# A hybrid decoder trunk: products of two head pairs issued in turn, and a queue of its own for the gate products

## The chip, the cores and the metric

The kernel runs on one core of one Trainium2 chip. The metric is the device time of one execution in microseconds, smaller is better. The time before is the median of three runs. One further execution was profiled, and all rows below come from that one.

## The reference, cut to what matters

Two residual layers over 512 positions and a width of 2048. Each layer normalises x, multiplies it by one wide input matrix, feeds slices of the result to four mixers, multiplies the mixers' outputs by a gate, and projects back.

```python
def layer(x):
    h = rms_norm(x); p = h @ w_in              # 52 column blocks of 128
    y = concat(mla(p), s5(p), rwkv7(p), diff_attention(p))   # 4 x 512 wide
    return x + (y * silu(gate(p))) @ w_out     # 2048 x 2048

def rwkv_step(state, r, w, k, v, a, b):        # 8 heads of 64, one state 64 x 64 each
    sa = state @ a
    state = state * w + sa[:, None] * b + v[:, None] * k
    return state, state @ r
```

## The kernel before, in words

**Layout.** Features lie on partitions, the 512 positions on the free axis. Every large product is split into three float32r products (high and low part of each side, helper `three`, line 258 on): TensorE sees 128x128 weights and 512 columns. Small products are plain float32, which TensorE runs as two instructions each. The profile shows all products on line L126 and all transposes on L130, the two methods of `Clock`.

**Order on TensorE.** The class `Clock` writes TensorE's order out by hand. It counts a modelled time from the columns issued. The filler is the stream of big products: `in_proj` (52 column blocks of 16 steps per layer), then `partial` (output blocks over the first 12 of 16 inner steps, taken from the list `PART`, while the attention is still running), then `out_proj` (the rest). Small work is generators: each `yield 6.0` says that its next piece is due 6 modelled us later, and `Clock.run` slips it into the filler when it is due. The generators are `recurrent` (the RWKV heads), `others` (S5 tables, S5, GLU, the latent attention, the differential attention) and, in `out_proj` of the first layer, `tables` for the second one.

**Order on the other engines.** A scheduler orders DVE, ACT, POOL and the DMA issues of SP by priority in a simulated time. On the chip each of these queues runs strictly in order. Weights come through `weights`: a DMA into `raw`, an ACT copy to `wh` (L242), a DVE subtraction to `wl` (L243), with three buffers of each, at high priority. `late(i)` keeps an ACT or DVE instruction behind the latest such weight split.

**Chunk products of RWKV** (`rwkv_two`). A pass `d` handles two head pairs, `s` = 0 and 1. Pair `s` keeps its operands on partitions `TS[s]`, 0 to 63 or 64 to 127. Within a pair there are two heads `h`. For each `(s, h)` the keys BK of eight chunks are written by DVE (L598, L599) into one buffer, then 8 products of 64x128 keys with 128 columns of Q are issued in two halves `j`, each followed by two masked copies out of PSUM by DVE (L608, L610), then 8 transposes of BK, copied out by ACT (L615). The one buffer makes the second head's keys wait until the first head's products are done.

**Gate products.** The gate block is scaled out of PSUM (L1449), goes through tanh (L1450, L1451) and is either multiplied at once (`mix`) or, when the mixers are not yet there, stored to DRAM (gD, `early`) and loaded again by `mix_one`. `mix` loads the mixer output y into the one buffer `zr` (L1461), POOL multiplies (L1462), ACT writes the high part MH (L1463), DVE the low part ML (L1464). `mixing` calls `mix_one` at every fourth step of the filler.

**Sums of squares.** `sum_sq` squares on ACT (L469) and adds on POOL (L471). `absorb` calls it for every output block of the first layer and also writes the next layer's XH (L462) and XL (L463). `out_proj` walks the blocks m = 0 to 15 in order. A block that `partial` has begun has 4 inner steps left, another one 16.

Of the kernel before, what the change touches and what calls it, by code (L numbers as in the profile page):

```python
# [187 lines left out]
def trunk(ctx, tc, io, KT=16, depth=DEPTH):  # L188
# [45 lines left out]

    def weights(pl, src, n, bufs, first=0, into=None):

        w = WCOL
        with tc.high_priority(offset=first) if first else ExitStack():
            raw = pl.tile([128, w], F32, tag="raw", name="raw", bufs=bufs[0])
            SP.dma_start(out=raw[:, :n], in_=src)  # L240
            wh, wl = into or (pl.tile([128, w], F32R, tag=t, name=t, bufs=bufs[1]) for t in ("wh", "wl"))
            x = A.copy(out=wh[:, :n], in_=raw[:, :n])  # L242
            y = V.tensor_sub(out=wl[:, :n], in0=raw[:, :n], in1=wh[:, :n])  # L243
# [35 lines left out]
    def small(pl, srcs, nk, rh, rl, done, bufs=(1, 2)):  # L279

        nxt = weights(pl, srcs[0], nk * 128, bufs)
        for j in range(len(srcs)):
            wh, wl = nxt
            if j + 1 < len(srcs):
                nxt = weights(pl, srcs[j + 1], nk * 128, bufs)
# [53 lines left out]
    def s5_tables(pl, l, pace):  # L339
# [76 lines left out]
        for q in range(4):  # L416
# [38 lines left out]
            SP.dma_start(out=s5tab[l, q], in_=cs2.rearrange("p a g q -> p a (g q)"))  # L455


    def absorb(sp, k, x, pvt, sqs, eng=G):
# [5 lines left out]
        sum_sq(sp, sqs, x, k == 0, eng)  # L464

    def sum_sq(lp, sqs, src, first, eng=G):

        sq = sqs if first else lp.tile([128, S], F32, name="sq", tag="sq", bufs=2)[:, :src.free_size()]
# [40 lines left out]
    def rwkv_two(rp, P, l, d, lo_, z, yD):  # L509
# [12 lines left out]
        Qs, BKts, SVs, bvs, nDs = [], [], [], [], []  # L522
        for s in range(2):
# [68 lines left out]

            for h in range(2):
                hs = TS[h]
                if h == 0:
                    yield 6.0
                BK = rp.tile([128, 8, 128], F32, name="BK", tag="BK", bufs=1)
                late(V.tensor_tensor(out=BK[T, :, T], in0=c3(b)[hs], in1=c3(Ei)[hs], op=ALU.mult))  # L598
                late(V.tensor_tensor(out=BK[T, :, B], in0=c3(k2)[hs], in1=c3(Ei)[hs], op=ALU.mult))  # L599
                yield Y["bk0"] - 5.0 if h == 0 else Y["bk1"]  # L600
                for j in range(2):
                    s4 = slice(8 * h + 4 * j, 8 * h + 4 * j + 4)
                    ps = pb()
                    for i in range(4):
                        PE.matmul(ps[:, i * 128:(i + 1) * 128], lhsT=BK[T, 4 * j + i, :],
                                  rhs=Q[T, 8 * h + 4 * j + i, :], start=True, stop=True)
                    ps3 = ps.rearrange("p (c t) -> p c t", t=128)
                    V.tensor_tensor(out=NM[T, s4, :], in0=ps3[T],  # L608
                                    in1=maskS[T].unsqueeze(1).to_broadcast([64, 4, 128]), op=ALU.mult)
                    V.tensor_tensor(out=Q[B, s4, :], in0=ps3[B],  # L610
                                    in1=maskS[B].unsqueeze(1).to_broadcast([64, 4, 128]), op=ALU.mult)
                ps = pb()
                for c in range(8):
                    PE.transpose(ps[:, c * 64:(c + 1) * 64], BK[T, c, :], ident[T, T])
                A.copy(out=BKt[:, 8 * h:8 * h + 8].rearrange("p c f -> p (c f)"), in_=ps)  # L615
            nD = dram(f"nD{l}{p}", [64, 16, 64])
            SP.dma_start(out=nD, in_=NM[T, :, 0:64])
            nDs.append(nD)
# [9 lines left out]
            Qs.append(Q), BKts.append(BKt), SVs.append(SV), bvs.append(bvD)  # L628

# [263 lines left out]
    def s5_glu(gp, l, P, uD, ysD, out):  # L893
# [12 lines left out]

        nxt = load(0)
        for t in range(4):
# [27 lines left out]
        yield from small(gp, [io["w_glu"][l, t] for t in range(4)], 4, GH, GL, done)  # L936
# [32 lines left out]
    def low_rank_col(pl, sqs, n, rxc, name, mul):  # L969
# [3 lines left out]
        yield 9.0  # L973
# [11 lines left out]
    def load_split(pl, src, n, P, g, name):  # L985
# [12 lines left out]
        for t in range(n):  # L998
# [9 lines left out]
            if t + 2 < n:  # L1008
                rs.append(load(t + 2))
                yield 4.0  # L1010
        return xh, xl, sqs

    def mla_kv(pa, l, P, aD, rxc, knD, vtD):
        def at():
            return pa.tile([128, S], F32, name="at", tag="at", bufs=3)

        kh, kl, ksq = yield from load_split(pa, aD[0:2], 2, P, "kvg", "ck")
# [9 lines left out]
        yield from small(pa, [io["w_uk"][l, h] for h in range(4)], 2, kh, kl, done)  # L1027
        ws = [weights(pa, io["w_uv"][l, :, k * 512:k * 512 + 512], 512, (1, 2)) for k in range(2)]
# [10 lines left out]
    def mla_q(pa, l, P, aD, rxc, qnD, qrD):  # L1039
        qh, ql, sqs = yield from load_split(pa, aD[3:7], 4, P, "qg", "cq")  # L1040
# [3 lines left out]
        order = (4, 5, 0, 1, 2, 3)  # L1044
# [7 lines left out]
        yield from small(pa, [io["w_uq"][l, j] for j in order], 4, qh, ql, done)  # L1052
# [28 lines left out]
    def mla_att(pd, qc, qn, qnD, qrD, knD, kpD, vtD, out):  # L1081
        def raw(src):
            t = pd.tile([128, S], F32, name="raw", tag="raw", bufs=3)
# [15 lines left out]
        def head(h):  # L1099
            if h == 0:  # L1100
                r = raw(kpD)
                yield Y["ld"]
                hd["kp"] = split("kp", r)
                load(0)
                yield Y["ld"]
# [680 lines left out]
```

## Time and profile before

| | us |
|---|---|
| median of three runs | 2024.81 |
| lowest and highest | 2019.72, 2025.67 |
| the profiled execution, its own time | 2023.16 |
| its span | 2021.4 |

The profiled execution took 1.76 us more than its span, and lies 1.65 us below the median. Busy times of TensorE overlap: a 512-column product is shown with about 390 ns and the next one begins about 230 ns later. A gap is therefore read from one start to the next. The mean granted TensorE clock over the execution is 0.982 of full speed.

### The profile page before, as it was taken

To read this page: it belongs to the slowest core of one execution; us is meant where nothing else is said; L and a number is where in the kernel's file an instruction comes from. 1 tells how busy PE (TensorE), PEld (TensorE's weight loads), DVE (VectorE), ACT (ScalarE), POOL (GpSimd) and SP (SyncE) were. 2 spreads that over 40 slices of the span, in tenths; PEclk is the share of its full clock that TensorE was granted. 3 is DMA by queue.
4 is the path that set the end of the run, shared out by engine and by line. 5 is a ranking of instruction groups with operands and counts; after the bars stand their busy time and mean duration, and the time that the engine had idled before them with its cause. 6 is when DMAs were issued, how large, how long until landed. Compare 5 with 4: busy or idle time off the path is not lost.

```text
span 2021.4 us, 31452 instructions
## 1 busy us (share of the span) xinstructions
PE 1955.9 (97%) x10975; PEld 1596.9 (79%) x10975; DVE 1303.5 (64%) x2801; ACT 831.8 (41%) x1734; POOL 368.4 (18%) x422
## 2 busy tenths in 40 slices
PE   9979999999999999998999999999999998999997
PEld 7767877788888787886788888778787787887787
DVE  6886866546776577649646686664683675766442
ACT  5543434344234355434433233443332353554351
POOL 1112203123001122004101111312210112200122
PEclk9989989999999999998999999999999999999998
DMA  5453545455462455455642445365456437445553
GB/s 209 142 167 117 144 119 148 155 169 171 151 214 95 146 179 172 154 171 179 203 133 93 136 119 155 96 194 170 160 158 172 150 100 224 131 145 167 159 175 116
DMA packets 241422, 311.08 MB, mean 154 GB/s; under 512 B 83312, under 2 KB 109168, under 8 KB 241264
## 3 DMA queue, kind: packets, MB, share of 16 engines
q1 hardware_dynamic: 241120, 308.91, 49.3%
q8 instruction: 86, 1.41, 0.3%
q14 instruction: 72, 0.59, 0.1%
q10 hardware_dynamic: 144, 0.17, 0.0%
HBM read 235.75 MB, written 70.88 MB: 152 GB/s over the span
## 4 chain that ended last, share of the span: by engine, by line
PE 77%; DMA 8%; DVE 7%; ACT 3%; issue 2%; POOL 1%; SPq 1%; DVEq 0%; POOLq 0%; ACTq 0%
PE acc L126 57%; PE pb L126 18%; PE pb L130 2%; DVE wl L243 1%; DMA zr<-yD 1%; POOL stg L1462 1%; DMA raw<-in_w_out_dram 1%; DMA raw<-qkD 1%; ACT K L850 1%; DMA raw<-in_w_in_dram 1%; DMA T<-K 1%; DMA qs<-qrD 0%; SPq L854 0%; DMA xo<-xP 0%; DMA gD<-stg 0%
## 5 line engine op out<-in xcount | busy, mean ns | idle before, releaser
L126 PE MATMUL acc<-XH,wl 128*128 128x512 f32 x1600 | 654.8, 409 | 20.3 <-DVE zr L504 10.7
L126 PE MATMUL acc<-XL,wh 128*128 128x512 f32 x1600 | 629.9, 394 | 1.1 <-DVE XL L463 1.1
L126 PE MATMUL acc<-XH,wh 128*128 128x512 f32 x1600 | 629.9, 394 | 0.0
L242 ACT CAST wh<-raw 128x512 fp32r<-128x512 f32 (+1 forms) x560 | 342.4, 616 | 563.9 <-PE acc L126 415.9
L243 DVE TENSOR_TENSOR wl<-raw,wh 128x512 fp32r<-128x512 f32 (+1 forms) x560 | 395.3, 710 | 257.5 <-ACT wh L242 253.1
L126 PEld LDWEIGHTS acc<-XH,wl 128*128 128x128 f32 x1600 | 303.8, 190 | 95.2 <-DVE zr L504 11.2
L126 PEld LDWEIGHTS acc<-XH,wh 128*128 128x128 f32 x1600 | 303.1, 189 | 66.0
L126 PEld LDWEIGHTS acc<-XL,wh 128*128 128x128 f32 x1600 | 304.1, 190 | 60.7 <-DVE XL L463 2.7
L126 PE MATMUL acc<-MH,wl 128*128 128x512 f32 x448 | 180.9, 404 | 12.5 <-DVE xo L1545 10.1
L126 PE MATMUL acc<-ML,wh 128*128 128x512 f32 x448 | 176.5, 394 | 0.2 <-DVE ML L1464 0.2
L126 PE MATMUL acc<-MH,wh 128*128 128x512 f32 x448 | 176.5, 394 | 0.0
L703 POOL TENSOR_SCALAR tmp<-SV,ec 64x64 f32<-64x64 f32 x112 | 69.8, 625 | 339.8 <-DVE SV L730 171.7
L126 PEld LDWEIGHTS acc<-MH,wl 128*128 128x128 f32 x448 | 85.3, 190 | 32.7 <-DVE xo L1545 11.8
L126 PEld LDWEIGHTS acc<-MH,wh 128*128 128x128 f32 x448 | 85.0, 190 | 18.3
L126 PEld LDWEIGHTS acc<-ML,wh 128*128 128x128 f32 x448 | 85.3, 190 | 16.5 <-DVE ML L1464 0.5
L1462 POOL TENSOR_TENSOR stg<-stg,zr 128x512 f32<-128x512 f32 x32 | 45.7, 1428 | 178.3 <-DMA zr<-yD 67.4
L471 POOL TENSOR_TENSOR sqs<-sqs,sq 128x512 f32<-128x512 f32 (+1 forms) x32 | 42.3, 1321 | 133.6 <-ACT sq L469 133.5
L1279 POOL TENSOR_TENSOR sr<-ss,cc 128x1 f32<-128x1 f32 x32 | 21.8, 686 | 188.0 <-DVE ss L1277 178.2
L955 ACT ACTIVATE pt<-pb,nb,fc 128x128 f32<-128x128 f32 (+3 forms) x64 | 39.5, 618 | 32.9 <-DVE nb L954 32.5
L640 DVE TENSOR_TENSOR tmp<-X 64x30 f32<-64x30 f32 (+14 forms) x120 | 39.2, 326 | 11.0 <-DMA X<-nD 5.1
L953 DVE TENSOR_REDUCE mx<-pb 128x1 f32<-128x128 f32 (+3 forms) x96 | 45.9, 478 | 0.5
L1463 ACT ACTIVATE MH<-stg 128x512 fp32r<-128x512 f32 x32 | 20.1, 631 | 57.3 <-POOL stg L1462 50.5
(398 smaller groups left out, 2908.6 us busy)
## 6 DMA issues: line engine op xcount, KB each, us to landing
raw<-in_w_in_dram SPq DMA_DIRECT2D x416, 256.0 KB, 3.4
raw<-in_w_out_dram SPq DMA_DIRECT2D x128, 256.0 KB, 3.4
zr<-yD SPq DMA_DIRECT2D x32, 256.0 KB, 2.9
gD<-stg SPq DMA_DIRECT2D x22, 256.0 KB, 3.3
stg<-gD SPq DMA_DIRECT2D x22, 256.0 KB, 3.4
zD<-stg SPq DMA_DIRECT2D x18, 256.0 KB, 3.1
xP<-stg SPq DMA_DIRECT2D x18, 256.0 KB, 2.1
xo<-xP SPq DMA_DIRECT2D x18, 256.0 KB, 3.4
```

The lines of the kernel that those rows point to most:

```text
L126: return self.nc.tensor.matmul(out, lhsT=lhsT, rhs=rhs, **kw)
L130: return self.nc.tensor.transpose(out, in_, identity)
L242: x = A.copy(out=wh[:, :n], in_=raw[:, :n])
L243: y = V.tensor_sub(out=wl[:, :n], in0=raw[:, :n], in1=wh[:, :n])
L471: eng.tensor_tensor(out=sqs, in0=sqs, in1=sq, op=ALU.add)
L640: i = V.tensor_tensor(out=t2, in0=X[:, 0:j, j:j + 1].to_broadcast([64, j, n]), in1=X[:, j:j + 1, j + 1:32].to_broadcast([64, j, n]), op=AL ...
L703: G.tensor_scalar(out=T1[T, h], in0=SVs[s][T, c, h], scalar1=ec[T, h, c:c + 1], scalar2=None, op0=ALU.mult)
L850: A.copy(out=K[:, g], in_=ps[32 * g:32 * g + 16, 0:128])
L953: V.tensor_reduce(out=mx, in_=ps[:, 0:n], axis=AX.X, op=ALU.max)
L955: A.activation(out=pt, in_=ps[:, 0:n], func=AF.Exp, scale=fcol[:, qb:qb + 1], bias=nb, accum_out=sm)
L1279: G.tensor_tensor(out=sr, in0=ss, in1=C("mhalf", 0, 1), op=ALU.pow)
L1462: G.tensor_tensor(out=g, in0=g, in1=y, op=ALU.mult)
```

## The change

1. **Chunk products.** The products of both head pairs are taken out of the loop over `s` and issued after both pairs are prepared, in turn: pair 0, pair 1, pair 0, and so on, into two PSUM banks. The transposes likewise. The keys of the second head get a place of their own: that of the states SV, which are not needed yet.
2. **Gate products.** `mix`, `open_mix`, `mix_one` and `mixing` go. A generator `mixer` takes their place. Every gate block is stored to DRAM. The mixer loads y and gate for up to two tiles into four buffers, and 9 modelled us later issues the product on DVE, then MH and ML as before. `partial` now runs until all 16 tiles are mixed.
3. **Sums of squares** are added on DVE everywhere.
4. **Order of `out_proj`** in the first layer: full blocks and begun blocks alternate.
5. **Small weights** (`small`, `mla_kv`) are loaded two ahead and early, and split only when due. Some due times are shorter: 9 to 6 in `low_rank_col`, 4 to 3 in `load_split`, one wait of 9 less at the first attention head, tables at a pace of 3.0 in place of 4.5 in the second layer and of 2.5 in place of 3.0 in the first, with one pause more per quarter before their store.

```diff
+    def small(pl, srcs, nk, rh, rl, done, raws):
+        def split(j):
+            wh, wl, x, y = split_w(pl, raws[j], nk * 128, 2)
+            late(x)
+            if j + 2 < len(srcs):
+                raws.append(load_w(pl, srcs[j + 2], nk * 128, 2))
+            return wh, wl
...
-            SP.dma_start(out=s5tab[l, q], in_=cs2.rearrange("p a g q -> p a (g q)"))
+            yield pace
+            late(SP.dma_start(out=s5tab[l, q], in_=cs2.rearrange("p a g q -> p a (g q)")))
...
         if not first:
-            eng.tensor_tensor(out=sqs, in0=sqs, in1=sq, op=ALU.add)
+            V.tensor_tensor(out=sqs, in0=sqs, in1=sq, op=ALU.add)
...
+            yield 4.0
+            Ks.append((BK, SV.rearrange("p c h v -> p c (h v)")))
             for h in range(2):
                 hs = TS[h]
-                if h == 0:
-                    yield 6.0
-                BK = rp.tile([128, 8, 128], F32, name="BK", tag="BK", bufs=1)
-                late(V.tensor_tensor(out=BK[T, :, T], in0=c3(b)[hs], in1=c3(Ei)[hs], op=ALU.mult))
-                late(V.tensor_tensor(out=BK[T, :, B], in0=c3(k2)[hs], in1=c3(Ei)[hs], op=ALU.mult))
-                yield Y["bk0"] - 5.0 if h == 0 else Y["bk1"]
...
+                late(V.tensor_tensor(out=Ks[s][h][T, :, T], in0=c3(b)[hs], in1=c3(Ei)[hs], op=ALU.mult))
+                late(V.tensor_tensor(out=Ks[s][h][T, :, B], in0=c3(k2)[hs], in1=c3(Ei)[hs], op=ALU.mult))
...
+        yield 5.0
+        for h in range(2):
+            for j in range(2):
+                s4 = slice(8 * h + 4 * j, 8 * h + 4 * j + 4)
+                pss = pb(), pb()
+                for i in range(4):
+                    for s, T in enumerate(TS):
+                        PE.matmul(pss[s][:, i * 128:(i + 1) * 128], lhsT=Ks[s][h][T, 4 * j + i, :],
+                                  rhs=Qs[s][T, 8 * h + 4 * j + i, :], start=True, stop=True)
+                for s, T in enumerate(TS):
+                    B = TS[1 - s]
+                    ps3 = pss[s].rearrange("p (c t) -> p c t", t=128)
+                    V.tensor_tensor(out=NM[T, s4, :], in0=ps3[T],
+                                    in1=maskS[T].unsqueeze(1).to_broadcast([64, 4, 128]), op=ALU.mult)
+                    V.tensor_tensor(out=Qs[s][B, s4, :], in0=ps3[B],
+                                    in1=maskS[B].unsqueeze(1).to_broadcast([64, 4, 128]), op=ALU.mult)
+                yield 2.6
+            pss = pb(), pb()
+            for c in range(8):
+                for s, T in enumerate(TS):
+                    PE.transpose(pss[s][:, c * 64:(c + 1) * 64], Ks[s][h][T, c, :], ident[T, T])
...
+            if h == 0:
+                yield 1.0
...
-        yield 9.0
+        yield 6.0
...
-            G.tensor_tensor(out=g, in0=g, in1=y, op=ALU.mult)
...
+        def mixer(self, mctx):
+            l, on, n = self.l, [], 0
+            yield from self.need(("rwkv",))
...
+            while len(self.mixed) < 16:
+                t = next((t for t in self.gates if (l, "y", t) in PE.done), None)
+                if t is not None and len(on) < 2:
+                    self.gates.remove(t)
+                    (a, x), (b, z) = (((zp, "zr"), (cp, "w2a2")), ((mp, "y"), (cp, "lo")))[n % 2]
+                    y, g = (q.tile([128, S], F32, name=w, tag=w, bufs=1) for q, w in ((a, x), (b, z)))
+                    SP.dma_start(out=y, in_=self.yD[t])
+                    SP.dma_start(out=g, in_=self.gD[t])
+                    on.append((PE.t + Y["ld"], t, y, g))
+                    n += 1
+                elif on and on[0][0] <= PE.t:
+                    _, t, y, g = on.pop(0)
+                    late(V.tensor_tensor(out=g, in0=g, in1=y, op=ALU.mult))
+                    A.mul(out=self.MH[:, t], in_=g, mul=0.5)
+                    V.scalar_tensor_tensor(out=self.ML[:, t], in0=g, scalar=0.5, in1=self.MH[:, t],
+                                           op0=ALU.mult, op1=ALU.subtract)
+                    self.mixed.add(t)
+                yield 1.5
...
             for m in PART:
-                if (l, "others") in PE.done:
+                if len(self.mixed) == 16:
                     break
...
-            for m in range(KT):
+            order, rest = [], [m for m in range(KT) if m not in self.part]
+            for j, m in enumerate(rest):
+                order += [m] + self.part[j * len(self.part) // len(rest):(j + 1) * len(self.part) // len(rest)]
+            for m in order:
...
+                PE.spawn(L.mixer(mctx), 2)
```

## Rows read from the trace of the kernel before

**Rows 1.** The page's first part: busy us, share of the span, instructions.
```profile
PE 1955.9 (97%) x10975; PEld 1596.9 (79%) x10975; DVE 1303.5 (64%) x2801; ACT 831.8 (41%) x1734; POOL 368.4 (18%) x422
```

**Rows 2.** TensorE's waits: waiting line, releaser, us in total, times, longest.
```profile
PE acc L126 <- DVE zr L504: 10.7, 1, 10.7
PE acc L126 <- DVE xo L1545: 10.1, 4, 4.6
...
PE pb L126 <- DVE BK L599: 1.9, 1, 1.9
```

**Rows 3.** Stretches: PE, PEld, DVE, ACT, POOL busy; granted clock; DMA share; GB/s.
```profile
98.00:120.00 22.00, 11.27 (x41) 8.80 (x38) 17.10 (x30) 13.93 (x23) 4.58 (x6) 0.69 0.41 137
146.00:157.00 11.00, 9.12 (x38) 6.83 (x38) 7.20 (x11) 1.20 (x2) 1.66 (x2) 0.69 0.55 160
...
760.00:772.00 12.00, 7.74 (x28) 6.24 (x27) 8.82 (x26) 5.36 (x15) 4.00 (x4) 0.72 0.58 182
928.00:973.00 45.00, 33.80 (x126) 25.99 (x127) 45.00 (x117) 20.66 (x44) 10.35 (x6) 0.89 0.58 180
...
1694.00:1724.00 30.00, 23.49 (x92) 18.48 (x92) 17.53 (x27) 13.78 (x26) 9.01 (x6) 0.89 0.71 221
```

**Rows 4.** TensorE's groups of instructions for the chunk products and transposes.
```profile
L126 PE MATMUL pb<-Q,BK 64*128 64x128 f32 x256 | 33.2, 281 | 1.9 <-DVE BK L599 1.9
...
L130 PE MATMUL pb<-cc,BK 64*128 64x64 f32 x128 | 10.8, 227 | 0.0
```

**Rows 5.** TensorE in order of time, one head's chunk products: start, us, instructions.
```profile
139.14 2.05 PE L126 MATMUL pb<-Q,BK 64*128 64x128 f32 x16
141.03 0.65 PE L130 MATMUL pb<-cc,BK 64*128 64x64 f32 x8
141.61 0.50 PE L126 MATMUL acc<-XH,wl 128*128 128x512 f32 x1
```

**Rows 6.** TensorE in order of time: two products on partition halves, then one on all.
```profile
97.61 1.13 PE L126 MATMUL pb<-lo,w2a 64*128 64x512 f32 x4
...
477.60 1.12 PE L126 MATMUL pb<-rk,cc 128*128 128x512 f32 x2
```

**Rows 7.** All engines in order of time, a stretch of the first layer's output projection.
```profile
942.55 1.44 POOL L471 TENSOR_TENSOR sqs<-sqs,sq 128x512 f32<-128x512 f32 x1 [0.88 <-ACT sq L469]
942.75 1.79 DVE L463 SCALAR_TENSOR_TENSOR XL<-xo,pvt,XH 128x512 fp32r<-128x512 f32 x1
...
946.36 0.74 DVE L463 SCALAR_TENSOR_TENSOR XL<-xo,pvt,XH 128x512 fp32r<-128x512 f32 x1
```

**Rows 8.** All engines in order of time, gate products of the first layer.
```profile
754.98 1.28 POOL L1462 TENSOR_TENSOR stg<-stg,zr 128x512 f32<-128x512 f32 x1 [3.68 <-DMA zr<-yD]
756.29 0.63 ACT L1463 ACTIVATE MH<-stg 128x512 fp32r<-128x512 f32 x1 [3.30 <-POOL stg L1462]
...
766.16 0.58 PE L126 MATMUL pb<-dVT,PT 128*128 128x128 f32 x1 [4.26 <-ACT PT L965]
```

**Rows 9.** DVE's groups of instructions.
```profile
L610 DVE TENSOR_TENSOR Q<-pb,cc 64x512 f32<-64x512 f32 x32 | 22.0, 688 | 0.6
...
L1464 DVE SCALAR_TENSOR_TENSOR ML<-stg,MH 128x512 fp32r<-128x512 f32 x32 | 21.9, 688 | 30.7 <-ACT MH L1463 30.6
```

**Rows 10.** POOL's groups of instructions, shapes apart.
```profile
L1462 POOL TENSOR_TENSOR stg<-stg,zr 128x512 f32<-128x512 f32 x32 | 45.7, 1428 | 178.3 <-DMA zr<-yD 67.4 <-DVE ss L1277 24.4 <-DMA stg<-gD 21.8
L471 POOL TENSOR_TENSOR sqs<-sqs,sq 128x512 f32<-128x512 f32 x26 | 37.9, 1456 | 114.9 <-ACT sq L469 114.7
```

**Rows 11.** DMA issues: engine, count, KB each, median us to landing.
```profile
raw<-in_w_in_dram SPq DMA_DIRECT2D x416, 256.0 KB, 3.4
...
gD<-stg SPq DMA_DIRECT2D x22, 256.0 KB, 3.3
```

**Rows 12.** All engines in order of time, the query compression's sum of squares.
```profile
487.74 2.98 POOL L1007 TENSOR_TENSOR sqs<-sqs,rw 128x512 f32<-128x512 f32 x2 [1.97 <-ACT rw L1006]
...
498.65 0.95 PE L126 MATMUL pb<-cc,sqs 128*128 128x2 f32 x8
```

More of the change, by code (lines that the diff above doesn't have):

```diff
@@ L232, in trunk, with load_w, split_w @@
     s5b = dram("s5b", [depth, 4, 128, 2, 2, 64])
-    def weights(pl, src, n, bufs, first=0, into=None):
[L237 to L243, printed above, removed]
+    def load_w(pl, src, n, bufs):
+        raw = pl.tile([128, WCOL], F32, tag="raw", name="raw", bufs=bufs)
+        SP.dma_start(out=raw[:, :n], in_=src)
+        return raw
+    def split_w(pl, raw, n, bufs, into=None):
+        wh, wl = into or (pl.tile([128, WCOL], F32R, tag=t, name=t, bufs=bufs) for t in ("wh", "wl"))
+        x = A.copy(out=wh[:, :n], in_=raw[:, :n])
+        y = V.tensor_sub(out=wl[:, :n], in0=raw[:, :n], in1=wh[:, :n])
+        return wh, wl, x, y
+    def weights(pl, src, n, bufs, first=0, into=None):
+        with tc.high_priority(offset=first):
+            raw = load_w(pl, src, n, bufs[0])
+            wh, wl, x, y = split_w(pl, raw, n, bufs[1], into)
             if first == AHEAD:
@@ L905, in load @@
             return u, y
+        srcs = [io["w_glu"][l, t] for t in range(4)]
         nxt = load(0)
+        raws = [load_w(gp, x, 512, 2) for x in srcs[:2]]
         for t in range(4):
@@ L934, in done @@
             out(4 + t, o)
-        yield from small(gp, [io["w_glu"][l, t] for t in range(4)], 4, GH, GL, done)
+        yield from small(gp, srcs, 4, GH, GL, done, raws)
     def softmax(pl, ps, qb, fcol, fneg, tag, bufs):
@@ L1025, in done @@
             SP.dma_start(out=knD[h], in_=t)
-        yield from small(pa, [io["w_uk"][l, h] for h in range(4)], 2, kh, kl, done)
-        ws = [weights(pa, io["w_uv"][l, :, k * 512:k * 512 + 512], 512, (1, 2)) for k in range(2)]
+        yield from small(pa, srcs, 2, kh, kl, done, raws)
+        raws = [load_w(pa, io["w_uv"][l, :, k * 512:k * 512 + 512], 512, 2) for k in range(2)]
+        yield 7.0
+        ws = []
+        for k in range(2):
+            wh, wl, x, y = split_w(pa, raws[k], 512, 2)
+            late(x)
+            ws.append((wh, wl))
         for t in range(4):
@@ L1039, in mla_q @@
     def mla_q(pa, l, P, aD, rxc, qnD, qrD):
+        order = (4, 5, 0, 1, 2, 3)
+        srcs = [io["w_uq"][l, j] for j in order]
+        raws = [load_w(pa, x, 512, 2) for x in srcs[:2]]
         qh, ql, sqs = yield from load_split(pa, aD[3:7], 4, P, "qg", "cq")
@@ L1050, in done @@
             SP.dma_start(out=qnD[j] if j < 4 else qrD[j - 4], in_=o)
-        yield from small(pa, [io["w_uq"][l, j] for j in order], 4, qh, ql, done)
+        yield from small(pa, srcs, 4, qh, ql, done, raws)
         return qc, qn
@@ L1312, in tables @@
         with sub("tab", l) as st:
-            yield from s5_tables(st, l, 3.0 if l == 0 else 4.5)
+            yield from s5_tables(st, l, 2.5 if l == 0 else 3.0)
         PE.done.add((l, "tab"))
@@ L1487, in mixing @@
-        def mixing(self, mctx, products):
-            for i, x in enumerate(products):
-                if i % 4 == 2:
-                    self.mix_one(mctx)
-                yield x
-        def partial(self, mctx):
+                SP.dma_start(out=self.gD[t], in_=g)
+                self.gates.append(t)
+            self.finish(n, t)
+        def mixer(self, mctx):
+            l, on, n = self.l, [], 0
+            yield from self.need(("rwkv",))
+            mp = mctx.enter_context(sub("mix", l, side="right"))
+            self.MH = mp.tile([128, 16, S], F32R, name="MH")
+            self.ML = mp.tile([128, 16, S], F32R, name="ML")
+            while len(self.mixed) < 16:
[16 more added lines that the diff above has]
+                yield 1.5
@@ L1669, in everything @@
             with ExitStack() as mctx:
-                yield from L.in_proj(mctx, begun)
+                PE.spawn(L.mixer(mctx), 2)
+                yield from L.in_proj(begun)
                 begun = []
-                yield from L.partial(mctx)
-                while L.early or (l, "others") not in PE.done:
-                    if not L.mix_one(mctx):
-                        yield False
+                yield from L.partial()
+                while len(L.mixed) < 16:
+                    yield False
                 with sub("wp", l) as wp:
```

95 lines of the change are left out of this document (28 added, 67 removed).

## The prediction

> **What bounds the kernel now.** I read the page's engine table first, then TensorE's waits, then single stretches of the trace. The table shows TensorE busy for 97% of the span and DVE for 64% [rows 1]. So only two things can make the kernel faster: less work on TensorE, or the few stretches in which TensorE stands still or runs at a lower clock. The list of waits names the first kind of stretch: one wait of 10.7 us at the start for an evacuation of PSUM, four of together 10.1 us in the output projection for L1545, and 1.9 us for the second head's keys [rows 2]. The stretches show what lies around them [rows 3]. Length less busy time is idle time. A granted clock of 0.72 is a mix of the two levels 2.4 and 1.2 GHz; length times one minus the clock is the most that the lower level can have cost (less where idle time falls into it). This gives, idle plus clock:
>
> - 98 to 120 us, start of the first layer: 10.7 + 6.8
> - 146 to 157, the wait for the keys: 1.9 + 3.4
> - 760 to 772 and 1694 to 1724, gate products: 4.3 + 3.4 and 6.5 + 3.3, together 17.5
> - 928 to 973, output projection of the first layer: 11.2 + 5.0 = 16.2
>
> In all of them TensorE's idle time precedes the lower clock or lies in it, so what ends the wait is taken to give the clock back too.
>
> **Chunk products in turn.** There are 256 instructions of products and 128 of transposes [rows 4]; at 16 and 8 to a head that is 16 blocks (two layers, two passes, two pairs, two heads). One block takes 141.03 - 139.14 = 1.89 us for the products and 0.58 for the transposes [rows 5], 2.47 in all, so 39.5 us of TensorE's time. Each product uses only 64 of 128 partitions, one after the other on the same half. What alternating halves do is shown elsewhere in this trace: two products of 512 columns on the two halves, four instructions, take 1.13 us, and one such product on all partitions, two instructions, takes 1.12 [rows 6]. Two halves cost as much as one. If the new order gets the same, 39.5 becomes 19.8. The new pauses break each pass into six stretches in place of four, eight more in all; a 512-column product behind such a block shows 0.50 us in place of the usual 0.39 [rows 5], so 8 x 0.11 = 0.9. I take **-18**. No paired transpose is in the trace: if these gain nothing, 16 x 0.29 = 4.6 of it goes. Ends: 0 (nothing side by side) and -20.
>
> The wait for the keys goes, since both heads' keys have a place. I take **-3** of 1.9 + 3.4; ends 0 and -5, because the due times around it are new. Keys of pair 0 now wait until pair 1 is prepared. That costs TensorE nothing as long as big products fill in. The pauses of a pass were 2 x (6 + 4.55 + 4.2) = 29.5 modelled us and are 2 x 4 + 5 + 4 x 2.6 + 1 = 24.4, so the chain behind does not start later.
>
> The same masked copies by DVE remain, 64 of 0.688 us (L610 and its twin L608) [rows 9]. Four of them, 2.75 us, now follow 0.95 us of products in place of two after 0.95. Six PSUM banks and 2.6 us of other work lie between two halves, so I price this at nothing. The Trainium skill speaks against that: TensorEngine Tiling (Array Packing), section PSUM Bottleneck, says that tiling speeds up TensorE and not the evacuation, which may become the limit. By that rule the sum below would be -9 in place of -38; it is the second rival.
>
> **Gate products.** Before, ACT's high part MH stands in order behind POOL, POOL behind the one buffer zr: POOL waited 3.68 us for the DMA, MH 3.30 for POOL, and TensorE at the end of that chain 4.26 us for a PT copy queued on ACT [rows 8]. The weights' copies stand on the same ACT queue. In the second layer the same chain holds the evacuation of PSUM. The mixer waits 9 modelled us between load and use, against a landing of about 3.4 us [rows 11], with two pairs of buffers, so nobody waits in line. Of 17.5 I take **-13**; ends 0 and -17.5. What the mixer adds: ten gates more go through DRAM (32 in place of 22 [rows 11]), 20 DMAs of 256 KB, with SP's queue behind them (third rival). The last gates come about 10.5 modelled us later (9 + 1.5); `partial` then begins one or two further blocks, which is moved and not added work as long as its list of 12 lasts. If the list ran out, up to 10.5 us a layer would stand open.
>
> **From POOL to DVE.** 32 gate products and 32 adds leave POOL, 1428 and 1456 ns each at full size [rows 10]. On DVE an instruction of this shape with two inputs takes 0.69 (L1464) [rows 9], so 44 us more, DVE at 68% of a shorter span. Against it: while POOL added at 942.55 for 1.44 us, DVE's XL took 1.79 us, and 0.74 once POOL was still [rows 7]. So an add on POOL cost DVE up to 1.05 where it met an instruction with two inputs, more than the add itself on DVE. I put the exchange at 0 outside the output projection.
>
> **Output projection.** DVE is busy for 45.0 of the 45 us from 928 to 973 [rows 3]: it is the limit there, not TensorE. A begun block takes 12 products, at 0.23 us 2.8 us of TensorE, and three DVE instructions, 0.69 + 0.69 + 0.74 = 2.1. Three in a row leave the tables little, and the tables are queued ahead of L1545, which frees the accumulator. A full block leaves about 7 us of 11. Alternating, 13.8 us of TensorE meet 5 x 0.69 + 2 x (0.69 + 0.74 + 0.69) = 7.7 us of DVE, with the added sums in. But the tables' pace goes from 4.5 to 3.0, so half as much again of their work comes per us. I take back half of 16.2, **-8**; ends 0 and -16.
>
> **Edits at nothing.** The first layer's start (10.7 + 6.8) keeps its parts: tables, the first head pair and the evacuations meet on ACT and DVE. A pace of 2.5 with 22 pauses is 55 us, 3.0 with 18 was 54. I take 0; ends -17 and +5. The shorter due times are covered: the query's sum was ready at 490.72 and used at 498.65 [rows 12], 7.9 us for 3 + 2 taken away. Without the cover, the 5 us would show four times in part. For this and for waits that a new order brings anywhere (each of the present ones is 1 to 5 us) I add **+4**; ends 0 and +15. Early loads of small weights are hidden as before.
>
> **Sum.** -18 - 3 - 13 - 8 + 4 = -38 on the profiled execution's own 2023.2 gives 1985.2. The median of the runs lies 1.6 above it, so 1986 to 1987; I give **1986**.
>
> **Rivals.**
> 1. *The waits change place.* Pairing works, but DVE with 44 us more, and tables at a faster pace, holds the same instructions: the 8 and 13 do not come. 1986 + 21 = 2007. For it: DVE full for 45 us. Against it: the waits in the gate products are an order of waiting, not a load (DVE 17.5 of 30 us there [rows 3]).
> 2. *Evacuation takes over.* Each of 16 halves holds TensorE for 2.75 in place of 0.95 us: +29, so 2015. Against it: the six banks and the pause.
> 3. *Slower: the gates' round trip blocks SP.* A load of a gate can only start when its store has landed, 3.3 us [rows 11]. If it stands at the head of SP's queue, the weights behind it wait. A quarter of a block (12 products) lasts 2.8 us; two quarters in store make 5.5, less the landing of 3.4 and two conversions of about 0.65 leaves 0.8 of cover. So each blocked gate costs TensorE 2.5 us. The gain of 38 is gone when 15 of the 32 are blocked; with 20 it is 1986 + 50 = 2036. Against it: the same loads of y behind their stores are in the kernel before.
> 4. *No pairing.* The halves don't overlap in this form (128 columns, two banks): 1986 + 18 = 2004. Rows 6 speak against it.
>
> **Chances and range.** Forecast 0.58 (own range 1966 to 2003), rival 1 0.15, rival 2 0.12, rival 3 0.08, rival 4 0.06, anything else slower 0.01. The range from 1963 to 2015 leaves out rival 3, part of rival 2 and the lower ends together, about 0.18. Three runs of before span 0.3%, which is about what a measurement can tell from no change. Below 2018.7 lie the forecast, rivals 1 and 4 and two thirds of rival 2: faster 0.86. Within 0.3%: 0.05, from rivals 2 and 3. Slower: 0.09.
>
> **What the profile would show.** Right: 16 chunk instructions in about 0.95 us in place of 1.89, with starts in pairs; no wait for BK; MH no longer waiting for POOL; POOL's busy time down by some 88 us and DVE's up by less than 44; waits for L1545's successor under 8 us. Wrong: chunk products still 118 ns apart; a wait of TensorE for PSUM copies behind each half; SP waiting for the landing of gD with `raw` behind it; the tables crowding DVE again.

## The result, and the profile after

The changed kernel is slower. Its median is 2037.94 us (2036.15 to 2047.21, 5 runs), beside 2021.67 us (2017.6 to 2025.67, 5 runs) for the kernel before: ratio 1.0089 [1.006, 1.0118], the brackets being a 95% interval. The forecast was 1986, and no rival had this cause. The profiled execution has an own time of 2036.15 us and a span of 2034.3, 13.0 us above the execution that the sum was made against. Of the four executions of the kernel of experiment 1 below, one took 5891.77 us and is a slow run; it is left out of every comparison, so that this kernel's median is that of the three others.

The page's engine table of after, beside [rows 1]:

```profile
PE 1946.9 (96%) x10975; PEld 1581.4 (78%) x10975; DVE 1325.9 (65%) x2865; ACT 833.8 (41%) x1734; POOL 273.5 (13%) x358
```

TensorE's busy time fell by 9.0 us and its span grew by 12.9, so some 22 us more are idle. POOL's busy time fell by 94.9 us and DVE's rose by 22.4. TensorE's waits of after, as in [rows 2] (waiting line, releaser, us in total, times, longest):

```profile
PE pb L126 <- DVE rk L617: 45.6, 8, 10.2
PE acc L126 <- DVE zr L520: 10.7, 1, 10.7
PE pb L126 <- ACT IN L869: 3.5, 9, 0.8
PE pb L126 <- DVE tmp L689: 2.5, 2, 1.3
PE pb L126 <- ACT PT L994: 1.9, 5, 0.8
PE pb L126 <- DVE wr L1669: 1.9, 1, 1.9
PE acc L126 <- DVE xo L1575: 1.8, 1, 1.8
...
PE acc L126 <- DVE wl L244: 1.1, 3, 0.6
```

The waits that the change aimed at are gone or small. The 10.1 us for xo in the output projection are 1.8 + 0.9 (L1575 and L1592), and no wait for BK is left. In their place stands a wait that the kernel before didn't have: 45.6 us in eight waits, all for L617. L617 writes r times r_k times the key, DVE's input to the *bonus product*, `pbn = pb()` and the matmul with `bones` behind it. There is one such product in each pair, pass and layer, which makes eight. The page's group of it:

```profile
L126 PE MATMUL pb<-rk,cc 128*128 128x512 f32 x16 | 15.9, 1094 | 45.6 <-DVE rk L617 45.6
```

Windows around the eight products show what that cost (columns as in [rows 3]):

```profile
128.00:152.00 24.00, 17.36 (x65) 12.45 (x63) 17.66 (x26) 4.85 (x8) 5.03 (x7) 0.86 0.83 222
168.00:182.00 14.00, 9.09 (x30) 6.35 (x29) 10.41 (x15) 1.39 (x3) 3.28 (x2) 0.76 0.17 53
...
498.00:515.00 17.00, 6.78 (x22) 4.53 (x22) 13.27 (x14) 2.91 (x5) 7.71 (x6) 0.70 0.20 60
...
sum 118.00, PE 72.41 PEld 50.13 DVE 83.26 ACT 17.20 POOL 34.50; mean PE 9.05 PEld 6.27 DVE 10.41 ACT 2.15 POOL 4.31
```

118.00 - 72.41 = 45.6 us are idle. The granted clock is 0.70 to 0.86 there, a mix of the levels 2.4 and 1.2 GHz. Length times one minus the clock, over all eight windows, is 25.3 us, at most, because idle time falls into it.

The longest of the eight in DVE's order of time (start, us, instruction), with TensorE's product at the end:

```profile
498.75 3.35 DVE L601 SCALAR_TENSOR_TENSOR Q<-tmp,E 64x512 f32<-64x512 f32 x2
...
503.98 1.63 DVE L614 TENSOR_TENSOR BK<-tmp 64x512 f32<-64x512 f32 x1
505.62 1.66 DVE L614 TENSOR_TENSOR SV<-tmp 64x512 f32<-64x512 f32 x1
507.31 0.69 DVE L806 TENSOR_TENSOR stg<-acc,rxr 128x512 f32<-128x512 f32 x1
507.92 0.68 DVE L244 TENSOR_TENSOR wl<-raw,wh 128x512 fp32r<-128x512 f32 x1
508.64 0.68 DVE L615 TENSOR_TENSOR BK<-tmp 64x512 f32<-64x512 f32 x1
509.33 0.69 DVE L615 TENSOR_TENSOR SV<-tmp 64x512 f32<-64x512 f32 x1
510.04 0.75 DVE L617 SCALAR_TENSOR_TENSOR rk<-rk,pvt,tmp 128x512 f32<-128x512 f32 x1
...
510.94 2.05 PE L126 MATMUL pb<-rk,cc 128*128 128x512 f32 x2 [10.22 <-DVE rk L617]
```

DVE has no idle time from 498.75 to 510.79. The four key writes and L617 come one behind the other, and no pause stands between them and the product; the only one, of 4 modelled us, stands ahead of the key writes. TensorE takes its instructions in the order written out, so the big products behind it wait too. The product itself then takes 2.05 us at a granted clock of 0.50, where it took 1.12 at full clock before [rows 6]. In the kernel before the same product stood behind both heads' chunk products, with 6 + 4.55 + 4.2 = 14.75 modelled us of pauses between its inputs and itself, and showed no wait. Part of the delay is POOL's: two key writes take 1.63 and 1.66 us in place of 0.68, while POOL runs these (order of time, same kernel):

```profile
503.69 1.37 POOL L1036 TENSOR_TENSOR sqs<-sqs,rw 128x512 f32<-128x512 f32 x1 [2.14 <-ACT rw L1035]
505.03 1.71 POOL L608 TENSOR_TENSOR tmp<-rk,tmp 128x512 f32<-128x512 f32 x1
```

The Trainium skill, SBUF — State Buffer, section Who interferes with whom, says that a DVE instruction with two SBUF inputs contends with a POOL instruction that reads SBUF, and that the one issued later blocks. The two rows agree: about 1 us for each of the two writes.

What the change was said to do to the chunk products is there. Their groups, beside [rows 4] (the second head's keys are named SV now):

```profile
L126 PE MATMUL pb<-Q,BK 64*128 64x128 f32 x128 | 9.3, 285 | 0.0
L126 PE MATMUL pb<-Q,SV 64*128 64x128 f32 x128 | 9.3, 285 | 0.0
...
L130 PE MATMUL pb<-cc,BK 64*128 64x64 f32 x64 | 2.9, 229 | 0.0
L130 PE MATMUL pb<-cc,SV 64*128 64x64 f32 x64 | 2.8, 229 | 0.0
```

18.6 + 5.7 = 24.3 us in place of 33.2 + 10.8 = 44.0. From the first start of each block to the start of what follows, summed over all blocks and without waits, it is 22.7 us in place of 40.3, so the saving is 17.6 us. One block in order of time, beside [rows 5]:

```profile
183.80 1.16 PE L126 MATMUL pb<-Q,BK 64*128 64x128 f32 x16
188.52 1.16 PE L126 MATMUL pb<-Q,BK 64*128 64x128 f32 x16
193.24 0.72 PE L130 MATMUL pb<-cc,BK 64*128 64x64 f32 x16
```

TensorE's account closes. The lines of its list of waits add up to 55.6 us before and 77.5 after: 45.6 are new, and 23.7 net are gone from the rest, above all 7.4 (xo, 10.1 to 1.8 and 0.9), 6.0 (ACT's PT, 7.9 to 1.9), 5.2 (the gate block's evacuation, L1449 before), 4.2 (wl, 5.3 to 1.1) and 1.9 (keys). Idle time so grew by 21.9 us, busy time fell by 9.0, and the difference of 12.9 is what the span grew by. Busy time fell by less than the 17.6 of the products because other instructions took longer: the bonus products alone went from 10.0 to 15.9 us, standing behind the eight waits at a lower clock. The mean clock over the span went from 0.982 to 0.975.

### The profile page after: what moved, and what is told of

It reads as the page before. It is cut to its first block, busy times and chain, and to the rows that moved or that the text cites. A ratio compares the mean times of both kernels' runs of the same rounds, so it can differ in the third digit from the quotient of the medians.

```text
span 2034.3 us, 31417 instructions
## 1 busy us (share of the span) xinstructions
PE 1946.9 (96%) x10975; PEld 1581.4 (78%) x10975; DVE 1325.9 (65%) x2865; ACT 833.8 (41%) x1734; POOL 273.5 (13%) x358
## 4 chain that ended last, share of the span: by engine, by line
PE 78%; DVE 8%; DMA 6%; ACT 3%; issue 2%; SPq 1%; POOL 1%; DVEq 0%; ACTq 0%; POOLq 0%
PE acc L126 59%; PE pb L126 16%; PE pb L130 2%; DVE wl L244 2%; DMA raw<-in_w_out_dram 1%; DMA raw<-in_w_in_dram 1%; DVE SV L614 1%; DVE Q L601 1%; DVE tmp L667 1%; ACT K L877 1%; DVE X L671 0%; DMA qs<-qrD 0%; SPq L237 0%; DMA X<-nD 0%; DMA T<-K 0%
## 5 line engine op out<-in xcount | busy, mean ns | idle before, releaser
L126 PE MATMUL acc<-XH,wl 128*128 128x512 f32 x1600 | 658.9, 412 | 12.5 <-DVE zr L520 10.7
L243 ACT CAST wh<-raw 128x512 fp32r<-128x512 f32 x560 | 342.4, 616 | 634.4 <-PE acc L126 502.3
L244 DVE TENSOR_TENSOR wl<-raw,wh 128x512 fp32r<-128x512 f32 x560 | 382.9, 687 | 262.8 <-ACT wh L243 251.2
L126 PEld LDWEIGHTS acc<-XH,wl 128*128 128x128 f32 x1600 | 304.7, 190 | 87.6 <-DVE zr L520 11.2
L730 POOL TENSOR_SCALAR tmp<-SV,ec 64x64 f32<-64x64 f32 x112 | 65.4, 585 | 353.2 <-DVE SV L757 180.8
L126 PE MATMUL pb<-rk,cc 128*128 128x512 f32 x16 | 15.9, 1094 | 45.6 <-DVE rk L617 45.6
L981 DVE TENSOR_TENSOR pb<-pb,cc 128x128 f32<-128x128 f32 x96 | 26.6, 295 | 24.5 <-PE pb L126 22.8
```

The costliest lines, as they stand in the source:

```text
L126: return self.nc.tensor.matmul(out, lhsT=lhsT, rhs=rhs, **kw)
L730: G.tensor_scalar(out=T1[T, h], in0=SVs[s][T, c, h], scalar1=ec[T, h, c:c + 1], scalar2=None, op0=ALU.mult)
L981: V.tensor_tensor(out=ps[:, qb * 128:n], in0=ps[:, qb * 128:n], in1=C("neg"), op=ALU.add)
```

## The experiments

Theory A: the bonus product, moved ahead of the chunk products with nothing to cover its input, costs all that was lost. Theory B: it is a mark on the chain, and another edit (evacuation, gates, tables) would hold TensorE there if it were gone. Theory C came with the pauses: passes that end later push the gates' work into the attention's stretch. Every ratio is to the kernel before on the chip of that experiment; four chips were used, with medians of the kernel before from 2018.96 to 2019.82. Differences in us between experiments are between medians.

**1. A pause ahead of the bonus product.**

```
             V.scalar_tensor_tensor(out=r, in0=r, scalar=P("r_k", p), in1=k2, op0=ALU.mult, op1=ALU.mult)
+            yield 8.0
             pbn = pb()
             PE.matmul(pbn, lhsT=bones, rhs=r, start=True, stop=True)
```

> The changed kernel with a pause of 8 modelled us between the bonus sum's DVE step (r times k2) and its product on TensorE, in both head pairs. Theory A (the moved product stands in TensorE's queue ahead of big products that could run, until DVE has worked off four key writes): the eight waits of together 45.6 us go, and part of the lower clock around them (at most 25 us more), so 2038 - 46 - 8 = 1984, between 1967 and 1992. Theory B (DVE has too much to do in these stretches, and the wait is only where this shows first): the wait moves to the chunk products or the weights, less than half comes back, above 2014.

1994.45 us (three runs), 0.9885 [0.9861, 0.9908]: 43.5 us under the changed kernel by the medians, 41 by the ratios, by one line. No wait for rk is left in TensorE's list, the bonus products take 8.2 us in place of 15.9, and the mean clock of the profiled execution is 0.985 in place of 0.975. Theory A holds, though the time lies a little above its band.

**2. The moved product in the kernel before.** The kernel before, with nothing changed but the place of r's product and of the two steps that take up its result (cut here): straight behind the first head's key writes.

```
             late(V.tensor_tensor(out=BK[T, :, B], in0=c3(k2)[hs], in1=c3(Ei)[hs], op=ALU.mult))
+            if h == 0:
+                V.scalar_tensor_tensor(out=r, in0=r, scalar=P("r_k", p), in1=k2, op0=ALU.mult, op1=ALU.mult)
+                pbn = pb()
+                PE.matmul(pbn, lhsT=bones, rhs=r, start=True, stop=True)
...
-            V.scalar_tensor_tensor(out=r, in0=r, scalar=P("r_k", p), in1=k2, op0=ALU.mult, op1=ALU.mult)
-            pbn = pb()
-            PE.matmul(pbn, lhsT=bones, rhs=r, start=True, stop=True)
```

> The kernel before with one thing moved: the bonus sum's DVE step and product come straight behind the first head's key writes instead of behind all chunk products. Theory A: the same wait appears in the kernel before, 8 times some 4 us plus the clock, so 30 to 55 us slower than before, 2050 to 2077. Theory B (it takes DVE's added work of the change to make the wait): less than 10 us slower.

2038.63 us, 1.01 [1.008, 1.0119], 19 us more. That is less than theory A said and more than B. Its waits name the same mechanism at a smaller size. Two things can make it smaller, and they were not parted: only one head's keys (two writes, not four) stand ahead of r, and the pause ahead of them is 6, not 4.

```profile
PE pb L126 <- DVE rk L601: 16.6, 8, 4.6
```

**3. How much pause.** The pauses ahead of the key writes and ahead of the chunk products were shortened, with the pause of 8 kept, then that pause was halved. The first edit:

```
-            yield 4.0
+            yield 2.0
...
-        yield 5.0
+        yield 1.0
```

> The changed kernel with the pause of 8 ahead of the bonus product, and two pauses of the change shortened (4 to 2 ahead of the key writes, 5 to 1 ahead of the chunk products), so that a pass has 32.4 modelled us of pauses (29.5 before the change, 40.4 in the run with the pause). Theory C (a pass that ends later bunches the gate products with the attention): first gate products about 8 to 16 us earlier than in the run with the pause and the time lower by 3 to 12 us, 1984 to 1993. If the length of a pass does not matter: within 3 us of 1996.

1989.3 us, 0.9853 [0.9834, 0.9872]: the best version found, 5 us under the first experiment (the runs do not overlap, the two intervals do a little), 30 under the kernel before and 49 under the changed one. In the trace the first gate product on DVE comes at 739.1 us and 1674.1 us in the two layers, in place of 747.5 and 1703.5 with the longer pauses. The direction and the time fit theory C, though the second layer's 29 us are more than it said; that the earlier gates are the cause is not shown. Engine table and waits:

```profile
PE 1934.5 (97%) x10975; PEld 1573.3 (79%) x10975; DVE 1320.0 (66%) x2864; ACT 833.1 (42%) x1734; POOL 270.3 (14%) x358
```

```profile
PE acc L126 <- DVE zr L520: 10.7, 1, 10.7
PE acc L126 <- DVE wl L244: 5.9, 5, 2.5
PE acc L126 <- DVE xo L1593: 4.2, 3, 2.7
...
PE pb L126 <- ACT PT L995: 2.4, 5, 1.1
```

The second edit, on top of the first:

```
-            yield 8.0
+            yield 4.0
```

> The kernel of the short pauses with 4 in place of 8 modelled us of pause ahead of the bonus product. The wait of that product was 5.7 us on average over eight in the changed kernel, with 4 modelled us of cover ahead of the key writes. If a pause shifts the product by about its own length, each of the eight still waits 1 to 3 us: the time rises by 6 to 20 us, ratio 0.988 to 0.995, and waits for r stand in TensorE's list. If the key writes run while other work covers them and only the last 2 to 3 us were missing: within 3 us, ratio 0.984 to 0.987.

2019.02 us, 1.0006 [0.9996, 1.0016], 29.7 more. That is past the upper end of both guesses, 20 us.

```profile
PE pb L126 <- DVE rk L617: 23.7, 8, 5.1
```

The modelled pause between r's other inputs and the product is 4 in the changed kernel, 2 + 4 here, 2 + 8 and 4 + 8 in the two others. The waits for rk are 45.6, 23.7, 0.3 us and none. The first two us of cover are worth 21.9 / 8 = 2.7 us for each product. The time moved by more than the 23.4 us of waits between these two kernels. In the slower one TensorE also waited 5.7 us for ACT's PT, 3.3 more; the other 3.0 are not accounted for.

**4. The value of taking the pairs in turn.** With the pause of 8 in place, the first pair's products and transposes emitted ahead of the second's; first with the longer pauses, then with the short ones.

```
-                for i in range(4):
-                    for s, T in enumerate(TS):
+                for s, T in enumerate(TS):
+                    for i in range(4):
...
-            for c in range(8):
-                for s, T in enumerate(TS):
+            for s, T in enumerate(TS):
+                for c in range(8):
```

> As the kernel with the pause, but the chunk products and transposes of pair 0 are all issued before those of pair 1. If the two partition halves run side by side when issued in turn, this one is slower than the kernel with the pause by 13 to 20 us, products again about 112 ns apart. If pairing gives nothing, the two are within 4 us.

> The kernel of the short pauses with the chunk products and transposes of the first pair emitted ahead of the second's, in place of in turn. The instructions themselves should take 11 us more in all (measured so between the two kernels with the longer pauses, which were 4.7 us apart in time). Theory H (pairing is worth what TensorE's rows show, the rest was lost to the later passes): the time rises by 9 to 14 us, ratio 0.990 to 0.992. Theory I (part of what pairing saves is lost in any case to other limits): 3 to 7 us, ratio 0.987 to 0.989.

2000.79 us, 0.9914 [0.9896, 0.9932], 6.3 more than with pairs in turn, which fits neither of its two expectations and whose interval overlaps; and 1998.85 us, 0.9906 [0.9891, 0.9921], 9.5 more. The groups in the second:

```profile
L126 PE MATMUL pb<-Q,SV 64*128 64x128 f32 x128 | 13.7, 285 | 0.0
L126 PE MATMUL pb<-Q,BK 64*128 64x128 f32 x128 | 13.7, 285 | 0.0
L130 PE MATMUL pb<-cc,SV 64*128 64x64 f32 x64 | 4.1, 229 | 0.0
L130 PE MATMUL pb<-cc,BK 64*128 64x64 f32 x64 | 4.0, 228 | 0.0
```

35.5 us against 24.3: taking them in turn saves 11.2 us of TensorE, and with the short pauses 9.5 of it arrive in the time, as theory H said. The other 8.5 of the 19.7 that the groups lost against the kernel before are there without taking turns, when each block holds four products of one half and then four of the other; why that is already shorter is not shown.

**5. The same piece alone in the kernel before.** Chunk products in turn, the second head's keys in the states' place and the pause of 8, all else as before; with the longer and with the short pauses.

> The kernel before with only the chunk products of the change (in turn, second keys in the states' place), with the pause of 8 us ahead of the bonus product. Theory A with the sum of the prediction: -18 for the products and -3 for the key wait, 2001, between 1996 and 2006. Theory B: the later and denser masked copies on DVE make waits of their own, 2012 or more.

> The kernel before with only the chunk products in turn, and the same shortened pauses. Theory C: the gain of 18 us on the products, which the run with the long pauses gave back, shows now, 1998 to 2008. If the gain was lost to something else than the later end of the passes, the time stays within 4 us of that run, 2014 to 2022.

2017.92 us, 0.9995 [0.998, 1.001], and 2016.01 us, 0.9983 [0.9973, 0.9993]. The products shrink as in the whole change (24.3 us in both), and the time gains nothing or 3 us. The shorter pauses did not bring the 18 us back here, so theory C fails in this kernel. Waits of the second:

```profile
PE acc L126 <- DVE wl L243: 11.6, 11, 2.4
...
PE acc L126 <- DVE xo L1557: 9.7, 3, 5.5
PE pb L126 <- ACT PT L977: 9.4, 6, 4.0
```

wl rose from 5.3 to 11.6 us and PT from 7.9 to 9.4, and the 10 us for xo stayed: without the other pieces, DVE and ACT hold TensorE again. But the evacuation's 5.2 us went, and the whole list rose by only 4.0, from 55.6 to 59.6. The two profiled executions are 10.5 us apart in span, more than the medians: this one is the fastest of its ten, and that of the kernel before lies 4 us above the median measured beside it. So the traces can't say where the gain of the products went, and this stays open.

**6. The output projection's order.** The first experiment's kernel with full and begun blocks not alternating.

```
-            for m in order:
+            for m in range(KT):
```

> The changed kernel with the pause of 8, and the first layer's output projection walked in the order 0 to 15 again (sums still on DVE). If the order brought the gain there: 8 to 16 us slower than with the pause alone, 2004 to 2012, with waits for the accumulator again. If moving the sums to DVE did it: within 3 us of 1996.

1996.95 us, 0.9894 [0.9874, 0.9915], 2.5 more than with the order and the same within the noise. The waits for xo are 2.2 us here and 2.5 with the order. It is worth nothing that can be told here.

**7. The sums' engine.** The kernel of the short pauses, with all sums of squares added on POOL (also those of the input, which the kernel before added on DVE).

```
-            V.tensor_tensor(out=sqs, in0=sqs, in1=sq, op=ALU.add)
+            G.tensor_tensor(out=sqs, in0=sqs, in1=sq, op=ALU.add)
```

> The kernel of the short pauses (0.9853 of the time before) with the sums of squares added on POOL again, as the kernel before had them. Theory D (the sums' move to DVE made the output projection's gain, because an add on POOL holds up DVE's instructions with two inputs): the waits for the output projection's xo come back to 8 us or more, POOL's busy time rises by about 45 us, and the time rises by 6 to 12 us, ratio 0.988 to 0.992. Theory E (the exchange is worth nothing, the gain in the output projection comes from other edits): within 3 us, ratio 0.984 to 0.987, waits for xo stay under 4 us.

1993.2 us, 0.9877 [0.9863, 0.9892], 3.9 more; the two intervals overlap, and the ratio lies just between the bands of the two theories. The waits for xo are 3.8 us in both lines together, where they were 5.3, so theory D falls: the sums' move did not make the output projection's gain. POOL's adds cost DVE's XL what was read in [rows 7], the median XL of the input taking 1.56 us in place of 0.76; TensorE's waits for XL rose by only 1.1 us.

**8. The mixer.** First the old path of the gates in the first experiment's kernel; then, in the kernel of the short pauses, the mixer kept but its product on POOL.

```
-                    late(V.tensor_tensor(out=g, in0=g, in1=y, op=ALU.mult))
+                    late(G.tensor_tensor(out=g, in0=g, in1=y, op=ALU.mult))
```

> The changed kernel with the pause of 8, but the gate products as before the change (at every fourth step of the filler, one buffer, multiplied on POOL, no round trip where the mixer's output is there). By the prediction's term the mixer is worth 13 of at most 17.5 us: 2005 to 2014. If the round trip and DVE's added work eat that up: within 4 us of 1996 or below.

> The kernel of the short pauses with the mixer kept, but its product of gate and output on POOL in place of DVE. Theory F (the mixer's loads ahead of use made its gain of 8 us, the engine of the product is of no weight): within 3 us, ratio 0.984 to 0.987. Theory G (the engine counts too): the time rises by 4 to 9 us, ratio 0.987 to 0.990, with TensorE's waits growing in the stretches in which gates are multiplied.

2004.38 us, 0.993 [0.9911, 0.9949], with ten runs from 1997.88 to 2016.02. So the mixer is worth some 9 us there (9.9 by the medians, 9.1 by the ratios), and TensorE's waits for PT are 13.1 us without it and 3.8 with it. With the product on POOL: 2015.78 us, 0.9987 [0.9974, 0.9999], 26.5 more than with the short pauses, far past both theories, and slower than the old path even though that one had the longer pauses. One gate in order of time:

```profile
1754.27 0.33 SPq L1510 DMA_DIRECT2D lo<-gD  x1
...
1757.63 1.26 POOL L1515 TENSOR_TENSOR lo<-lo,y 128x512 f32<-128x512 f32 x1 [9.74 <-DMA lo<-gD]
...
1758.93 0.63 ACT L1516 ACTIVATE MH<-lo 128x512 fp32r<-128x512 f32 x1 [4.76 <-POOL lo L1515]
1759.46 0.25 ACT L995 COPY PT<-pb 128x128 f32<-128x128 f32 x1
...
1759.76 0.49 PE L126 MATMUL pb<-dVT,PT 128*128 128x128 f32 x2 [3.67 <-ACT PT L995]
```

This is the chain of [rows 8] again: MH stands on ACT in front of PT's copy while its gate is still on the way from DRAM. The call `late` places an instruction behind the weights' conversion of the moment, and it keeps a mark for ACT and DVE only. On POOL it does nothing. Two more runs part the two: the product on POOL with MH placed late, and the product on DVE without `late`.

```
-                    late(V.tensor_tensor(out=g, in0=g, in1=y, op=ALU.mult))
-                    A.mul(out=self.MH[:, t], in_=g, mul=0.5)
+                    late(G.tensor_tensor(out=g, in0=g, in1=y, op=ALU.mult))
+                    late(A.mul(out=self.MH[:, t], in_=g, mul=0.5))
```

```
-                    late(V.tensor_tensor(out=g, in0=g, in1=y, op=ALU.mult))
+                    V.tensor_tensor(out=g, in0=g, in1=y, op=ALU.mult)
```

> The kernel of the short pauses with the gate product on POOL, as in the run before, but with MH's copy on ACT placed behind the weights' conversions of the moment. If the loss of 26 us came from MH standing on ACT ahead of its data: most of it comes back, ratio 0.984 to 0.990, and TensorE's waits for ACT's PT fall from 18 us to under 6. If POOL itself makes it: ratio 0.995 to 1.001 again.

> The kernel of the short pauses with the gate product on DVE, but without the order behind the weights' conversions. If the order is what counts: the product stands on DVE ahead of its data too, TensorE's waits for ACT's PT rise to 10 us or more, and the ratio is 0.993 to 1.001. If POOL is what counts: within 3 us of the kernel of the short pauses, ratio 0.984 to 0.987.

2007.36 us, 0.9948 [0.9931, 0.9965], and 2023.98 us, 1.002 [1.0011, 1.0029], past even the upper end of the band for the order. Without `late` the same product on the same engine costs 34.7 us. DVE's waits of that kernel, then of the kernel of the short pauses:

```profile
DVE w2a L1515 <- DMA w2a<-gD: 15.6, 11, 3.1
DVE lo L1515 <- DMA lo<-gD: 15.1, 9, 3.1
DVE lo L1515 <- DMA y<-yD: 10.4, 5, 3.6
DVE w2a L1515 <- DMA zr<-yD: 6.2, 2, 3.8
```

```profile
DVE lo L1515 <- DMA y<-yD: 1.7, 2, 1.0
```

27 waits of together 47.3 us with `late` gone; with it four, of 1.7 us here and 1.5 for zr. So the mixer gains only with this order (2023.98 us without it, 2004.38 with the old gates): without it, loading 9 modelled us ahead does not hide the round trip through DRAM. The product on POOL with MH placed late got back a third of its loss (8.4 of 26.5); PT's waits fell from 18.1 to 7.3 us, while wl's rose from 9.3 to 14.0. The rest may be POOL's own, which is argued and not shown: its product took 1.38 us on average in the run before, in place of 0.69, and with MH placed late DVE's ML waits 11.0 us for MH, where it was 4.8 with the product on DVE. Neither expectation fits that run alone.

## Why the prediction was wrong

**The step that failed** is in the part on the chunk products: "Keys of pair 0 now wait until pair 1 is prepared. That costs TensorE nothing as long as big products fill in." The keys do wait at no cost. But the chunk products that left this place had been the cover of the bonus product behind them, and with them gone it stands straight behind four key writes and its own input. The step looked at what was moved and not at what then became its neighbour. The +4 for new waits was the term that should have held it; it measured 45.6 us of waits, three times its upper end of 15, and 5.9 us more of slower bonus products. "So the chain behind does not start later" compared the sums of the pauses (29.5 and 24.4) and didn't ask which instruction stands behind which pause. Experiments 1 and 3 show the cause: with a pause put in, the wait and the loss go, and they come back in part with half of it. Experiment 2 shows the mechanism by itself.

**Chunk products, -18.** Right in TensorE's rows (17.6 from start to start; a block's 16 products take 1.09 us so, a little above the 0.95). Not borne out as a term of the sum: alone in the kernel before it brought 0 to 3 us, in the kernel of the short pauses the turn brought 9.5 of its 11.2. How much of a saving on TensorE arrives in the time depended on the other pieces.

**Key wait, -3.** The wait of 1.9 us is gone; what its clock gave back was not read.

**Gate products, -13.** It measured some 9 in the kernel with the pause, with the sign and place right (PT's waits 13.1 to 3.8 us). The reason given, 9 modelled us between load and use, was incomplete: `late`, which the prediction never named, holds 34.7 us. The statement that nobody waits in line did not hold: MH still waits 28.5 us for DVE's product in the changed kernel (21.0 and 7.5 for the two buffers), against 50.5 for POOL's before; only little of it reaches TensorE. The exchange of POOL for DVE at 0 looks too low: with MH placed late, the product on POOL costs 18 us, the sums 3.9, the latter hardly beyond the noise.

**Output projection, -8.** In the first layer's output projection TensorE's waits fell from 11.4 us to 1.8, by 9.6 where 8 was taken, but not for the reason given: neither the order (experiment 6) nor the sums (7), each taken back alone, brought the waits for xo back. With the old gates these are 4.4 us, in the kernel before with only the chunk products in turn 9.7. The tables' pace, the early loads and the new end of `partial` are what is left; they weren't tried apart, and this stays open.

**The start** kept its 10.7 us, as said.

**Rivals.** *The waits change place* describes experiment 5, not the result. *Evacuation takes over*: the rule of the Trainium skill (TensorEngine Tiling (Array Packing), section PSUM Bottleneck), stated there for a fourfold speedup, does not decide here, where two halves alternate; no wait of TensorE for the masked copies (L639, L641) stands in its list. *The gates' round trip blocks SP*: SP did wait for the stores, 15.5 us in ten waits, longest 2.8, where some 37 of TensorE's were needed to undo the gain:

```profile
SPq L1509 <- DMA gD<-stg: 15.5, 10, 2.8
```

TensorE's waits for wl, where that would show, fell to 1.1 us. *No pairing*: refuted by the rows. With the pause put in, the kernel of the short pauses stands at 1989 us, near the forecast; that is luck in part, since its terms are other ones than the sum had. One slip of the working changes nothing: the chances named for a faster kernel add up to 0.87, not 0.86.

## What to carry to other kernels

In an engine's written-out order, an edit that moves a block also uncovers what stood behind it: for each instruction left behind, ask what writes its input, when that ends, and what now lies between. Price a small product there at the wait of everything queued behind it, and look whether one pause gives it back before judging the rest. Saved busy time on the bounding engine is an upper bound, to be measured with the other pieces in place, because the chunk products' whole edit was worth 0 to 3 us alone, where taking the pairs in turn was worth 9.5 in the mended kernel.

## What the runs showed of the hardware

Products of 64 partitions that alternate halves took 1.16 us for 16 instructions (128 columns each, two banks) where one half alone took 2.05 [rows 5], both at full clock; transposes of 64 columns gained likewise, 0.72 us for 16 beside 0.65 for 8. Around eight standstills of 4.3 to 10.2 us the granted clock of the stretches was 0.70 to 0.86; the longest ended at a clock of 0.50, and the product behind it took 2.05 us in place of 1.12. The mean over the span was 0.975 with the standstills and 0.985 with the pause that removed them. POOL operations with two inputs beside DVE instructions with two inputs more than doubled these, as before [rows 7]: 1.63 and 1.66 us for key writes of 0.68.
